# Seven products over four chunks instead of two, in the first gate and up group and the last down group of a SwiGLU layer

## The chip, the cores and the metric

The kernel runs on one core of a Trainium2 chip. The metric is the device time of one execution in microseconds. The kernel before has a median of 1612.01 us over three runs, from 1611.77 to 1614.13.

## The reference, cut to what matters

One layer of a decoder, 256 tokens (T) of width D = 2048, all in fp32. Three token mixers, each with its own branch projection, are merged by gates and go through `w_o`; a SwiGLU layer of inner width FF = 5632 follows:

```python
x = x + merged @ w_o
h2 = rmsnorm(x, ffn_norm)
gate, up = split(h2 @ w_gate_up, 2)      # 2048 -> 2 x 5632
x = x + (silu(gate) * up) @ w_down       # 5632 -> 2048
```

## The kernel before, in words

**A product in fp32.** Each operand is split in two parts that TensorE multiplies fast, high and low: for a weight, `split` casts it on ScalarE (ACT, L151, tile `wh`) and subtracts the cast from it on VectorE (DVE, L152, tile `wl`). A product of a chunk of 128 inputs is then three matmuls, each 128 x 128 by 128 x 512: x high by w high (L268), x high by w low (L270), x low by w high (L271).

**A group.** `sgemm` computes two blocks of 512 output columns (j = 0, 1) for the two tiles of 128 tokens (t = 0, 1), over all chunks of the inner dimension: 16 for gate and up (one gate block and the up block beside it), 12 in the last part of the down product. Weights come by DMA as raw tiles of four chunks, 1 MB each. They are worked on in halves of two chunks: one cast of 128 x 1024, one subtraction, then the matmuls. The six raw tiles and six pairs `wh`, `wl` are rings: a new load waits until an old tile has been read for the last time.

**Seven products.** For the first eight chunks of a group the kernel can use the Strassen–Winograd form. The inner dimension is cut into two times SP = 4 chunks, so that the weights are four raw tiles: 11 and 21 (the two inner halves for block 0), 12 and 22 (for block 1). Seven products instead of eight give the four outputs; in the code they are the steps `p1`, `p2`, `p3`, `q4`, `p5`, `p6`, `p7`. Some of them need sums of activations, the *forms* (tiles `sh`, `sl`), which `make_forms` makes once for the whole product from `hh` and `hl`; others need sums or differences of weights, made in place in the raw tiles. The parameter `p` says how many of the four chunks of each half go this way: with p = 2 only the first two do, and the other two chunks of each raw tile go through the plain product (`rest`, in the lists l21, l22, l11, l12); the chunks after the first eight always do (r0 for block 0, r1 for block 1). One half of a step is 6 matmuls, one half of `rest` is 12, for it serves both token tiles.

**Sums of weights.** `prod` makes them on DVE ahead of the split of a half (L283): `p5` (21, 22), `p6` (21, 12), and `q4` (11, 21) where the group is `late` or not `moved`. Two sums go to the DMA queue of GpSimd (POOL) as accumulating transfers from one raw tile into another: `p6` adds 12 to 22 (L351) for `p7`, and in `moved` groups that aren't `late` `p2` adds 21 to 11 (L331) for `q4`. Both move `p` chunks. Such a transfer waits until the tile that it writes has had its last reader, and the cast that follows waits until it has landed.

**Three orders.** A list `seq` sets the order of the steps. The usual one is the last of the three in the code. In the first group of a product the forms aren't ready at the start, so `late` puts everything that needs none ahead: `p1`, `p2`, the plain halves, all of r0 and one of r1; then `made` runs what is left of the background work (here transposes of the normalized x, L455, L154, L155, and the forms, L418), and then come `p5`, `p6`, `p3`, `p7`, `q4` with the rest of r1 between. Its results go through pieces in SBUF, which L404 adds. The last group of the kernel has an order of its own, `end`: block 0's plain halves early, then `p5`, `p6`, `p2`, `p3`, `p7`, `q4`, and r1 at the very end. From these steps a scheduler makes the order of the instructions on each engine; an engine takes its instructions in that order, so one that waits holds up all behind it.

**Where the two groups stand.** The loop at L1130 runs gate and up groups i = 0 to 3, then the down product over those, then 4 to 7, then 8 to 10. Group i = 0 is `late`. The last down group (`end`) is the one for the last two blocks of the third part. The loop of w_o ahead of the FFN calls the same `sgemm` with p = SP, `late` in its first group.

Of the kernel before, what the change touches and what calls it, by code (L numbers as in the profile page):

```python
# [30 lines left out]
SP = KG  # L31
# [46 lines left out]
def trunk(ctx: ExitStack, tc: tile.TileContext, a, out):  # L78
# [109 lines left out]
    def piece():  # L188

        if kit is not None:  # L190
            return kit.tile([P, NB], F32, tag="cv", name="cv", bufs=8)
        if not halves:
            two = gog.tile([P, 2, NB], F32, name="two", tag="g_og")
            halves.extend([two[:, 1], two[:, 0]])
        return halves.pop()
# [214 lines left out]
    def form_tiles():  # L410
        return [fpool.tile([P, 4, SP, P], F32R, name=f"s{x}", tag=f"s{x}") for x in "hl"]

    def make_forms(parts, place):

        def add(dst, a, b, op=ALU.add):
            dve.tensor_tensor(dst, a, b, op=op)  # L418

        def make():  # L420
            a = {}
            for k in range(2):
                for i in range(2):
                    at = piece()
                    a[i, k] = at[:].rearrange("p (k t) -> p k t", k=SP)
                    n = 0
                    for h, l in parts:
                        m = h.shape[1]
                        lo, hi = max(k * SP, n), min((k + 1) * SP, n + m)
                        if lo < hi:  # L430
                            add(
                                a[i, k][:, lo - k * SP : hi - k * SP],
                                *(x[:, lo - n : hi - n, i * P : (i + 1) * P].bitcast(F32) for x in (h, l)),
                            )
                        n += m
                    yield
            a11, a12, a21, a22 = a[0, 0], a[0, 1], a[1, 0], a[1, 1]
            for f, dst, x, y, op in (
                (1, a21, a22, a21, ALU.subtract),
                (3, a22, a12, a22, ALU.subtract),  # L440
                (2, a12, a21, a12, ALU.subtract),
                (0, a11, a11, a12, ALU.add),
            ):
                add(dst, x, y, op)
                yield
                split(place[0][:, f], place[1][:, f], dst)
                yield
            making.remove(id(place))

        making.add(id(place))  # L450
        background.append(make())
        return place
# [96 lines left out]
    gain, i = {}, 0  # L549
# [439 lines left out]
    def to_chunks(src, n, hi, lo, gain):  # L989


        yield
        for c in range(0, 4, 2):
            p = tmp()
            for q in range(2):
                for t in range(2):
                    i = n + (c + q) * P
                    transpose(p[:, q * T + t * P : q * T + (t + 1) * P], src[t][:, i : i + P])
            if gain is None:
                split(*(x[:, c : c + 2].rearrange("p c t -> p (c t)") for x in (hi, lo)), p[:])  # L1000
            else:
                for q in range(2):
                    i = n // P + c + q
                    split(hi[:, c + q], lo[:, c + q], p[:, q * T : (q + 1) * T], gain[:, i : i + 1])
            yield
# [44 lines left out]
    for b in (2, 1, 0):  # L1050
# [3 lines left out]
        for n0 in range(0, D, 2 * NB):  # L1054
# [19 lines left out]
            for n, g in zip((n0, n0 + NB), gs):  # L1074
# [8 lines left out]
                part = [x[:, n // NB % 2 * 4 : n // NB % 2 * 4 + 4] for x in tm[-1]]  # L1083
# [30 lines left out]
    hs = [(hh[:, k], hl[:, k]) for k in range(KD)]  # L1114
# [13 lines left out]
    sf = make_forms([(hh, hl)], form_tiles())  # L1128
    NF = FF // NB
    for part in (range(0, 4), range(4, 8), range(8, NF)):  # L1130
        fs, tiles = [], []
        for i in part:
            for j, result in sgemm(hs, sf, a["w_gate_up"], (i, NF + i), 4 if i else 2, late=i == 0):
                if j == 0:
                    g = [piece()[:] for t in range(2)]
                    for t in range(2):
                        act.activation(g[t], result(t), AF.Silu, scale=r2[:, t : t + 1])
                    continue
                u = [piece()[:] for t in range(2)]
                for t in range(2):  # L1140
                    dve.scalar_tensor_tensor(u[t], result(t), r2[:, t : t + 1], g[t], op0=ALU.mult, op1=ALU.mult)
            f = [kit.tile([P, 4, T], F32R, name=f"f{x}", bufs=4) for x in "hl"]
            background.append(to_chunks(u, 0, *f, None))
            tiles.append(f)
            fs += [(f[0][:, k], f[1][:, k]) for k in range(4)]
            if len(tiles) == 2:
                sd = main.tile([P, 2, 4, SP, P], F32R, name="sd", tag="resid")
                sd = make_forms(tiles, [sd[:, 0], sd[:, 1]])
        final = part[-1] == NF - 1
        if final:  # L1150

            x2s = [fpool.tile([P, D], F32, tag=f"s{x}", name="x2s") for x in "hl"]
            for t in range(2):
                nc.gpsimd.dma_start(x2s[t][:], x2d[:, t])

        for n0 in range(0, D, 2 * NB):
            blks = (n0 // NB, n0 // NB + 1)
            end = final and n0 + 2 * NB == D
            base = (lambda j: x2s[1][:, n0 + j * NB : n0 + (j + 1) * NB]) if final else None
            for j, result in sgemm(  # L1160
                fs, sd, a["w_down"], blks, 2 if end else SP, row0=4 * part[0], moved=end, base=base, end=end
            ):
                n = n0 + j * NB
                for t in range(2):
                    if not final:
                        v = piece()
                        act.copy(v[:], result(t))
                        nc.gpsimd.dma_start(x2d[:, t, n : n + NB], v[:], accum_op=ALU.add)
                        continue

                    width = NB // 2 if n + NB == D else NB
                    for c in range(0, NB, width):
                        v = x2s[t][:, n + c : n + c + width]
                        dve.tensor_tensor(v, v, result(t)[:, c : c + width], op=ALU.add)
                        q = nc.scalar if (t, n + c + width) == (1, D) else nc.sync
                        q.dma_start(out[t * P : (t + 1) * P, n + c : n + c + width], v)
# [50 lines left out]
```

## Time and profile before

| | |
|---|---|
| median of three runs | 1612.01 us (1611.77 to 1614.13) |
| the profiled execution | 1609.67 us, of it span 1607.9 us |
| TensorE (PE) busy | 1600.4 us, 7204 instructions |
| VectorE (DVE) busy | 1354.9 us (84% of the span) |
| ScalarE (ACT) busy | 1043.8 us (65%) |
| first gate and up group on PE | 913.31 to 957.55 us of the span |
| last down group on PE | 1572.02 to 1603.74 us |

In a timeline row the first number is the start in the span, the second the time (of several alike, from the first one's start to the last one's end), then engine, line, operation, and out<-in; "x3" are three in a row, and what stands in brackets is the idle time before it and what ended it. In a row of windows each engine has its busy time and its number of instructions. For a DMA, "to landing" is the time from its issue until the data is there.

### The profile page before, as it was taken

The numbers are of one execution on the slowest core, as the hardware profiler recorded it, in microseconds if no ns is written. First come the engines' busy times: TensorE is split into PE (matmuls) and PEld (weight loads), VectorE is DVE, ScalarE is ACT, GpSimd is POOL, SyncE is SP. The second block draws the span as 40 slices with busy tenths as digits, with TensorE's granted clock in tenths as the row PEclk, the third lists the DMA queues.
The fourth block names the chain that finished last, engine by engine and source line by source line (L and its number), as shares of the span: only waits on it lengthen the run. The fifth ranks groups of instructions, "written<-read, shape, count | busy, mean of one in ns | idle before, by whom it ended". The sixth has DMA issues, their size and how long they took to land.

```text
span 1607.9 us, 19413 instructions
## 1 busy us (share of the span) xinstructions
PE 1600.4 (100%) x7204; PEld 1315.0 (82%) x7204; DVE 1354.9 (84%) x1544; ACT 1043.8 (65%) x1273; POOL 73.0 (5%) x95
## 2 busy tenths in 40 slices
PE   9999999999999999999999999999999999999998
PEld 7888888888888888888888888888888888888887
DVE  6777788897776788897799998988878988888996
ACT  7765677776764666665656766666666666666663
POOL 0000000000000000000000000000000000110000
PEclk9999999999999999999999999999999999999999
DMA  9765768767556878887757868777898786897684
GB/s 377 299 263 168 233 216 262 216 171 255 197 182 218 263 256 264 265 287 287 238 182 261 272 227 256 260 249 236 258 281 260 219 276 231 250 280 242 201 320 128
DMA packets 66383, 394.18 MB, mean 245 GB/s; under 512 B 7344, under 2 KB 14128, under 8 KB 21488
## 3 DMA queue, kind: packets, MB, share of 16 engines
q1 hardware_dynamic: 51344, 323.31, 52.5%
q0 software_dynamic: 11792, 66.59, 21.7%
q10 hardware_dynamic: 3152, 3.04, 0.6%
q8 instruction: 56, 0.92, 0.2%
q14 instruction: 39, 0.32, 0.1%
HBM read 324.24 MB, written 12.58 MB: 209 GB/s over the span
## 4 chain that ended last, share of the span: by engine, by line
PE 96%; DMA 2%; ACT 1%; DVE 1%; issue 0%; SPq 0%; DVEq 0%; ACTq 0%; POOLq 0%
PE acc L268 19%; PE acc L271 19%; PE acc L270 19%; PE tmp L271 7%; PE tmp L270 7%; PE tmp L268 7%; PE acc L226 5%; PE acc L225 5%; PE acc L224 5%; PE tmp L455 2%; DMA raw<-in_w_down 1%; DMA raw<-raw 0%; PE tmp L693 0%; PE tmp L721 0%; ACT wh L151 0%; DMA raw<-in_w_mem_kv 0%
## 5 line engine op out<-in xcount | busy, mean ns | idle before, releaser
L152 DVE TENSOR_TENSOR wl<-raw,wh 128x1024 fp32r<-128x1024 f32 (+1 forms) x765 | 920.1, 1221 | 209.9 <-ACT wh L151 196.6
L151 ACT CAST wh<-raw 128x1024 fp32r<-128x1024 f32 (+1 forms) x766 | 796.6, 1050 | 442.2 <-PE acc L271 225.5
L268 PE MATMUL acc<-wh,xTh 128*128 128x512 f32 x480 | 190.5, 397 | 0.0
L270 PE MATMUL acc<-wl,xTh 128*128 128x512 f32 x480 | 187.2, 390 | 0.0
L271 PE MATMUL acc<-wh,xTl 128*128 128x512 f32 x480 | 186.9, 390 | 0.0
L268 PE MATMUL acc<-wh,hh 128*128 128x512 f32 x452 | 178.8, 395 | 0.0
L270 PE MATMUL acc<-wl,hh 128*128 128x512 f32 x452 | 176.0, 389 | 0.0
L271 PE MATMUL acc<-wh,hl 128*128 128x512 f32 x452 | 175.0, 390 | 0.0
L283 DVE TENSOR_TENSOR raw<-raw 128x1024 f32<-128x1024 f32 x133 | 161.4, 1221 | 1.1 <-DMA raw<-in_w_down 0.5
L224 PE MATMUL acc<-wh,oh 128*128 128x512 f32 x320 | 126.6, 397 | 0.9 <-ACT wh L151 0.9
L225 PE MATMUL acc<-wl,oh 128*128 128x512 f32 x320 | 125.1, 391 | 0.5 <-DVE wl L152 0.5
L226 PE MATMUL acc<-wh,ol 128*128 128x512 f32 x320 | 124.8, 390 | 0.0
L268 PE MATMUL tmp<-wh,sh 128*128 128x512 f32 x294 | 115.7, 394 | 0.0
L271 PE MATMUL tmp<-wh,sl 128*128 128x512 f32 x294 | 114.7, 390 | 0.0
L270 PE MATMUL tmp<-wl,sh 128*128 128x512 f32 x294 | 114.6, 390 | 0.0
L268 PEld LDWEIGHTS acc<-wh,xTh 128*128 128x128 f32 x480 | 90.2, 188 | 20.7 <-ACT acc L314 3.1
L271 PEld LDWEIGHTS acc<-wh,xTl 128*128 128x128 f32 x480 | 90.1, 188 | 19.0
L270 PEld LDWEIGHTS acc<-wl,xTh 128*128 128x128 f32 x480 | 90.2, 188 | 17.8
L268 PEld LDWEIGHTS acc<-wh,hh 128*128 128x128 f32 x452 | 84.9, 188 | 18.6 <-ACT acc L314 1.0
L271 PEld LDWEIGHTS acc<-wh,hl 128*128 128x128 f32 x452 | 84.8, 188 | 18.0
L270 PEld LDWEIGHTS acc<-wl,hh 128*128 128x128 f32 x452 | 84.9, 188 | 16.8
L268 PE MATMUL acc<-wh,fh 128*128 128x512 f32 x220 | 86.5, 394 | 0.2 <-ACT acc L314 0.2
(311 smaller groups left out, 2322.1 us busy)
## 6 DMA issues: line engine op xcount, KB each, us to landing
raw<-in_w_gate_up SPq DMA_DIRECT2D x88, 1024.0 KB, 6.3
raw<-in_w_in SPq DMA_DIRECT2D x56, 1024.0 KB, 5.8
raw<-raw POOLq DMA_DIRECT2D x52, 1024.0 KB, 8.0
raw<-in_w_gate SPq DMA_DIRECT2D x48, 1024.0 KB, 7.4
raw<-in_w_down SPq DMA_DIRECT2D x44, 1024.0 KB, 7.2
raw<-in_w_o SPq DMA_DIRECT2D x16, 1024.0 KB, 6.2
raw<-in_w_mem_kv SPq DMA_DIRECT2D x14, 1024.0 KB, 10.5
raw<-in_w_br_mem SPq DMA_DIRECT2D x8, 1024.0 KB, 5.6
```

Source lines behind the costliest of these rows:

```text
L151: act.copy(hi, src)
L152: dve.tensor_tensor(lo, src, hi.bitcast(F32), op=ALU.subtract)
L224: pe.matmul(o[t][:], xh[:, s], wh[:, j], start=k == 0, stop=False)
L225: pe.matmul(o[t][:], xh[:, s], wl[:, j], start=False, stop=False)
L226: pe.matmul(o[t][:], xl[:, s], wh[:, j], start=False, stop=k == nk - 1)
L268: pe.matmul(dst[:], xh, wh, start=id(dst) not in begun, stop=False, skip_group_check=True)
L270: pe.matmul(dst[:], xh, wl, start=False, stop=False, skip_group_check=True)
L271: pe.matmul(dst[:], xl, wh, start=False, stop=last, skip_group_check=True)
L283: dve.tensor_tensor(x, x, y, op=ALU.add)
L455: pe.transpose(dst, src, ident)
```

## The change

Two arguments become `SP`, so that p = 4 in every group of the gate and up and the down product: in the first gate and up group (`late`), and in the last down group (`end`, the only one with `moved=True` in that loop).

```diff
-            for j, result in sgemm(hs, sf, a["w_gate_up"], (i, NF + i), 4 if i else 2, late=i == 0):
+            for j, result in sgemm(hs, sf, a["w_gate_up"], (i, NF + i), SP, late=i == 0):
...
             for j, result in sgemm(
-                fs, sd, a["w_down"], blks, 2 if end else SP, row0=4 * part[0], moved=end, base=base, end=end
+                fs, sd, a["w_down"], blks, SP, row0=4 * part[0], moved=end, base=base, end=end
             ):
```

In each of the two groups the steps p1 to p7 now work on two halves instead of one (12 matmuls each instead of 6), and the lists l21, l22, l11 and l12 are empty. That is 6 matmuls fewer a group and three split halves more (14 for the first eight chunks instead of 11). The gate group gets three more sums L283 (one each for p5, p6 and q4), the last group two more (p5 and p6). L351 in both groups and L331 in the last move 1 MB instead of 512 KB.

The first place is ACT at the start of the gate group. `wh_7682` is the cast of the first half of p1 in both; `xr` with `x2` is the sum of squares of the last w_o group. Before:

```order
L151 CAST wh_7740<-raw_7728 128x1024
L1108 ACTIVATE xr_7277,x2_ss_6912<-x2_7242 128x512
L1108 ACTIVATE xr_7275,x2_ss_6912<-x2_7242 128x512
L151 CAST wh_7767<-raw_7765 128x1024
L1108 ACTIVATE xr_7277,x2_ss_6912<-x2_7242 128x512
L151 CAST wh_7830<-raw_7810 128x1024
L151 CAST wh_7682<-raw_7680 128x1024
L151 CAST wh_7850<-raw_7848 128x1024
```

Now:

```order
L151 CAST wh_7734<-raw_7722 128x1024
L1108 ACTIVATE xr_7277,x2_ss_6912<-x2_7242 128x512
L1108 ACTIVATE xr_7275,x2_ss_6912<-x2_7242 128x512
L151 CAST wh_7755<-raw_7753 128x1024
L151 CAST wh_7818<-raw_7798 128x1024
L1108 ACTIVATE xr_7277,x2_ss_6912<-x2_7242 128x512
L151 CAST wh_7838<-raw_7836 128x1024
L151 CAST wh_7682<-raw_7680 128x1024
```

One cast (`wh_7838`, a plain half of r1) and the last L1108 have come between `wh_7818` and `wh_7682`. On TensorE 12 matmuls instead of 24 stand ahead of the first one that uses `wh_7682`.

The second place is DVE in the second half of the gate group. `raw_7680` is weight tile 21, `raw_7728` or `raw_7722` tile 11, `raw_7880` or `raw_7868` tile 22 and `raw_7927` or `raw_7910` tile 12; `sl` is a form. Before, from the sum of p6 on:

```order
L283 TENSOR_TENSOR raw_7680<-raw_7680,raw_7927 128x1024
L152 TENSOR_TENSOR sl_7673<-cv_7808,sh_7672 128x512
L152 TENSOR_TENSOR wl_7944<-raw_7927,wh_7943 128x1024
L152 TENSOR_TENSOR wl_7932<-raw_7680,wh_7931 128x1024
L152 TENSOR_TENSOR wl_7954<-raw_7927,wh_7953 128x1024
L152 TENSOR_TENSOR wl_7972<-raw_7969,wh_7971 128x1024
L152 TENSOR_TENSOR wl_7988<-raw_7880,wh_7987 128x1024
L283 TENSOR_TENSOR raw_7728<-raw_7728,raw_7680 128x1024
```

Now, from the second sum of p5 on:

```order
L283 TENSOR_TENSOR raw_7680<-raw_7680,raw_7868 128x1024
L152 TENSOR_TENSOR wl_7895<-raw_7836,wh_7894 128x1024
L283 TENSOR_TENSOR raw_7680<-raw_7680,raw_7910 128x1024
L152 TENSOR_TENSOR wl_7883<-raw_7680,wh_7882 128x1024
L283 TENSOR_TENSOR raw_7722<-raw_7722,raw_7680 128x1024
L152 TENSOR_TENSOR wl_7915<-raw_7680,wh_7914 128x1024
L283 TENSOR_TENSOR raw_7680<-raw_7680,raw_7910 128x1024
L152 TENSOR_TENSOR wl_7976<-raw_7868,wh_7975 128x1024
L283 TENSOR_TENSOR raw_7722<-raw_7722,raw_7680 128x1024
L152 TENSOR_TENSOR wl_7926<-raw_7680,wh_7925 128x1024
```

There are now two sums for each of p5, p6 and q4. `wl_7976` is the first half of p7, read from tile 22, into which L351 adds; it and a sum of q4 stand ahead of `wl_7926`, the second half of p6. On ACT the casts stand in the same order (`wh_7975` ahead of `wh_7925`), while on TensorE the matmuls of p6 come ahead of those of p7.

The third place is ACT at the end of the last group. `raw_13012` or `raw_13015` is tile 22, `raw_13058` or `raw_13067` tile 11, and `raw_13140` or `raw_13157` the last chunks, r1. Before:

```order
L151 CAST wh_13087<-raw_13027 128x1024
L151 CAST wh_13097<-raw_13027 128x1024
L151 CAST wh_13113<-raw_13012 128x1024
L151 CAST wh_13126<-raw_13058 128x1024
L151 CAST wh_13142<-raw_13140 128x1024
L151 CAST wh_13158<-raw_13140 128x1024
```

Now:

```order
L151 CAST wh_13090<-raw_13041 128x1024
L151 CAST wh_13100<-raw_13041 128x1024
L151 CAST wh_13110<-raw_13015 128x1024
L151 CAST wh_13120<-raw_13015 128x1024
L151 CAST wh_13175<-raw_13157 128x1024
L151 CAST wh_13133<-raw_13067 128x1024
L151 CAST wh_13143<-raw_13067 128x1024
L151 CAST wh_13159<-raw_13157 128x1024
```

p7 (`wh_13110`, `wh_13120`) and q4 (`wh_13133`, `wh_13143`) have two halves each, and a half of r1 (`wh_13175`) is now cast ahead of q4's, which waits for L331.

## The prediction

> **What bounds the kernel now.** I read the page first (busy time, and the chain of waits by engine), then the windows of the two places that change and of one place that already has the new form, then their timelines.
>
> ```profile
> PE 1600.4 (100%) x7204; PEld 1315.0 (82%) x7204; DVE 1354.9 (84%) x1544; ACT 1043.8 (65%) x1273; POOL 73.0 (5%) x95
> PE 96%; DMA 2%; ACT 1%; DVE 1%; issue 0%; SPq 0%; DVEq 0%; ACTq 0%; POOLq 0%
> ```
>
> TensorE (PE) is busy throughout and is 96% of the chain: as a rule a matmul fewer is a matmul's time won. VectorE (DVE) at 84% is an average, so it has to be read at the two places.
>
> ```profile
> core 0: us, PE busy (x) PEld busy (x) DVE busy (x) ACT busy (x) POOL busy (x), PEclk, DMA share, GB/s
> 832.00:874.00 42.00, 42.00 (x197) 34.80 (x195) 38.01 (x41) 26.23 (x34) 2.54 (x5) 1.00 0.74 245
> 913.30:937.00 23.70, 23.70 (x113) 19.46 (x112) 23.46 (x48) 16.26 (x27) 2.47 (x4) 1.00 0.58 170
> 937.00:957.40 20.40, 20.40 (x92) 16.90 (x91) 20.03 (x22) 13.83 (x16) 0.00 (x0) 1.00 0.70 277
> 1572.00:1603.70 31.70, 31.70 (x139) 25.63 (x137) 23.03 (x25) 11.91 (x13) 1.73 (x2) 1.00 0.36 107
> ```
>
> The second and third rows are the first gate and up group, the fourth the last down group, the first row the first group of w_o, which runs the same late order with p = 4 today. In the gate group PE has no gap, but DVE is busy 43.49 of 44.10 us: it is as full as PE. In the last group DVE has 8.67 us free, before the transfers that p6 and p2 start are counted.
>
> **The change part by part.** First the prices.
>
> ```profile
> 913.31 0.39 PE L268 MATMUL acc<-wh,hh 128*128 128x512 f32 x1
> 918.75 0.39 PE L268 MATMUL tmp<-wh,hh 128*128 128x512 f32 x1
> 937.15 0.39 PE L268 MATMUL tmp<-wh,sh 128*128 128x512 f32 x1
> 957.55 0.39 PE L268 MATMUL tmp<-wh,hh 128*128 128x512 f32 x1
> ...
> 1572.02 0.39 PE L268 MATMUL tmp<-wh,fh 128*128 128x512 f32 x1
> 1603.35 0.39 PE L271 MATMUL acc<-wh,fl 128*128 128x512 f32 x1
> ```
>
> These are the start of the gate group, its first matmul of p1, its first of p5, the first of the next group; then the last group's first matmul of p1 and the kernel's last matmul. From p5 to the next group the program has 90 matmuls: (957.55 - 937.15) / 90 = 0.2267 us each, the pitch of PE here.
>
> Removed: each of the two groups loses 6 matmuls (186 to 180 and 138 to 132), 2 x 6 x 0.2267 = 2.7 us if nothing else decides. Added, in each: three split halves (a cast on ScalarE, ACT, L151; a subtraction on DVE, L152), and three sums L283 in the gate group, two in the last. The POOL transfers L351 (one in each) and L331 (in the last) go from 512 KB to 1 MB.
>
> ```profile
> 929.00 1.22 DVE L283 TENSOR_TENSOR raw<-raw 128x1024 f32<-128x1024 f32 x1
> 930.13 0.69 DVE L418 TENSOR_TENSOR cv<-cv 128x512 f32<-128x512 f32 x1
> 939.62 5.76 DVE L152 TENSOR_TENSOR wl<-raw,wh 128x1024 fp32r<-128x1024 f32 x5
> 916.60 2.93 ACT L151 CAST wh<-raw 128x1024 fp32r<-128x1024 f32 x3
> ```
>
> The five in a row give DVE a pitch of (5.76 - 1.22) / 4 = 1.135 us for a sum or a split; a 512-wide operation takes about half of it (0.60 from start to start). The cast's pitch is (2.93 - 1.04) / 2 = 0.945, with 1.04 for a single one in the row at 914.22 below. So the gate group gets 6 x 1.135 = 6.8 us of DVE work where 0.6 us are free, and PE 1.36 us less. That cannot hide.
>
> ```profile
> 930.88 0.89 POOL L351 DMA_DIRECT2D raw<-raw  x1 [13.96 <-DVE cv L418]
> 1577.13 0.87 POOL L351 DMA_DIRECT2D raw<-raw  x1 [30.42 <-DVE raw L283]
> 1585.41 0.85 POOL L331 DMA_DIRECT2D raw<-raw  x1 [7.40 <-DVE wl L152]
> ...
> raw<-raw POOLq DMA_DIRECT2D x3, 512.0 KB, 4.6
> raw<-raw POOLq DMA_DIRECT2D x52, 1024.0 KB, 8.0
> ...
> DMA to landing us min/median/max: 5.5/5.5/5.5
> DMA to landing us min/median/max: 6.9/6.9/6.9
> DMA to landing us min/median/max: 4.6/8.8/10.6
> DMA to landing us min/median/max: 4.5/7.8/9.2
> ```
>
> These are the three 512 KB transfers, both sizes with their median from issue to landing, and four looks at the landing: the one at 930.88, the one of w_o's first group (1 MB, the same place in the same order), all of L351, all of L331. A transfer starts about 0.65 us after the DVE sum that it waits for (930.22 to 930.88). For 1 MB at the two places I take 7.0 us: by the w_o row, since both places have the lighter traffic that goes with it (shares 0.74 there, 0.70 and 0.36 here), under the median of 8.0. Bounds: 4.5 (as if it were still 512 KB) and 10.6.
>
> [...]
>
> Gate group, its start. p1 now takes four chunks, so only 12 matmuls, not 24, stand ahead of its first tmp matmul, while that half's cast still stands second behind an L1108 on ACT, which itself now stands behind one more cast.
>
> ```profile
> 914.22 1.04 ACT L151 CAST wh<-raw 128x1024 fp32r<-128x1024 f32 x1
> 915.97 0.63 ACT L1108 ACTIVATE xr<-x 128x512 f32<-128x512 f32 x1 [0.71 <-DVE x L1107]
> 914.12 1.22 DVE L152 TENSOR_TENSOR wl<-raw,wh 128x1024 fp32r<-128x1024 f32 x1
> ```
>
> Behind the cast of the first row another follows now, up to 916.2, then the L1108 to 916.9 (today it ends at 916.60); two casts behind it end at 916.9 + 2 x 0.945 = 918.8. PE gets there at 913.31 + 12 x 0.2267 = 916.0, held 0.45 by the split that ends at 915.34: it waits 2.4 us, and p1 starts at 918.9 instead of 918.75. From there to p5 both orders have 88 matmuls. So p5 starts at about 937.15 as before: the 12 matmuls (2.7 us) saved ahead are paid back in that wait, and 96 stand behind p5 instead of 90, which without a wait would end at 937.15 + 96 x 0.2267 = 958.9.
>
> Gate group, its middle. In DVE's new order nine operations of 1,024 columns and seven of 512 go from the first sum of p5 on (about 929.25, today 929.00) to the second sum of p6: 9 x 1.135 + 7 x 0.60 = 14.4, to 943.65. The transfer L351 waits for p5's second sum, which ends at 936.85, starts at 937.5 and lands at 944.5. On ACT the cast of p7, which waits for it, stands ahead of the cast for p6's second half, and on DVE p7's split and a sum of q4 stand ahead of that half's split. So: cast 945.6, then three operations on DVE, 945.6 + 3 x 1.135 = 949.0. PE comes to this half 30 matmuls behind p5's start and wants the low part at 937.15 + 32 x 0.2267 = 944.4. The wait is 4.7, with 0.2 of small ones behind it 4.9: end 963.8, against 957.55 **+6.3**. Queued behind that cast are those of p6, r1 and q4, and PE waits for all of them. With DVE alone (no landing awaited) the wait would be 2.7 and the sum +4.1; with a landing of 8.8 it is +8.1. The next group's splits have their lead of 4 to 5 us again by then, so I carry nothing over.
>
> Last group. Here DVE goes from 1573.03 through thirteen long operations (nine splits and four sums) and two short ones to the split that frees p2's chunks:
>
> ```profile
> 1573.03 2.36 DVE L152 TENSOR_TENSOR wl<-raw,wh 128x1024 fp32r<-128x1024 f32 x2
> 1585.57 3.49 DVE L152 TENSOR_TENSOR wl<-raw,wh 128x1024 fp32r<-128x1024 f32 x3
> 1590.02 2.95 ACT L151 CAST wh<-raw 128x1024 fp32r<-128x1024 f32 x3 [3.21 <-DMA raw<-raw]
> 1596.77 0.39 PE L268 MATMUL acc<-wh,fh 128*128 128x512 f32 x1
> ```
>
> 13 x 1.135 + 2 x 0.60 = 16.0, to 1589.0. On the way p6's first split is ready at 1584.4 where PE wants it at 1572.02 + 49 x 0.2267 = 1583.1: 1.2 us. L331 starts at 1589.65 (4.2 later than today's 1585.41) and lands at 1596.65. The third row shows the cast that waits for it today, 1590.02, and the fourth the matmul that uses the result, 1596.77: 4.7 us of cover once cast and split are taken off. That is gone: the cast ends at 1597.7, while q4 is due at 1603.35 - 1.36 - 35 x 0.2267 + 1.2 = 1595.3 (35 matmuls follow its first). Wait 2.4, then 1.0 for the split and 0.55 for the second half's, which stands behind two subtractions of p7. Sum 1.2 + 2.4 + 1.0 + 0.55 - 1.36 = **+3.8**. With a landing of 4.5 the 2.4 is nothing and it is +1.3; with 8.8 it is +5.6.
>
> Sum: 6.3 + 3.8 = +10.1; with both floors +5.4, with both landings of 8.8 +13.7. The profiled execution took 1609.67 (span 1607.9, the rest lies around it), 0.15% under the median of 1612.01; 1609.67 + 10.1 = 1619.8, and on the median 1622.1.
>
> **The rivals.** *All is covered* (the other side: faster by 2.7 us, 1609.3, which is 0.17%). For it speaks w_o's first group, the same late order with p = 4, without a gap on PE. Against it: that stretch leaves DVE 3.99 us free, while the gate group, whose DVE also makes hl and the forms (L155, L418), leaves 0.6. It decides only if the splits ran some 5 us further ahead than today's rows show.
>
> *The transfers land early.* If the 1 MB ones took about the 4.5 of a half, only the DVE waits stay: +5.4, 1617.4. For it: the two places have less traffic than the mean stretch. Against it: the shortest of all L351 is 4.6, and that is a 512 KB one; the only 1 MB row in a like place has 6.9.
>
> *The clock falls in the gap.*
>
> ```profile
> 1604.00:1608.00 4.00, 0.00 (x0) 0.00 (x0) 0.52 (x2) 0.00 (x0) 0.00 (x0) 0.85 0.32 107
> 1.19 4.45 PE L582 MATMUL tmp<-zeros 128*128 128x512 bf16 x10 [1.19 <-DVE zeros L579]
> ```
>
> PE stops at 1603.74; a granted clock of 0.85 over the 4 us means half speed for the last 1.2 us, about 3.1 us after PE went idle. The ten matmuls at the start take 0.43 us each, twice the pitch, for some 4.8 us. A gap over 3.1 us would then cost 2.4 more. In the forecast the 4.7 us wait is broken into 2.6, 0.9 and 1.2 by two matmuls (the cast comes before the split), so it stays under; with a landing of 8.8 the first piece is 4.4, and the sum +13.7 + 2.4 = 1628.1.
>
> [...]
>
> **How the numbers follow.** Forecast 0.70 (1622.1), early landings 0.15 (1617.4), fallen clock 0.07 (1628.1), all covered 0.08 (1609.3). The range of eight in ten goes from a little under the two floors, 1615.5, to between the landings of 8.8 (1625.7) and the fallen clock: 1627.5. A measurement of this kernel tells about 0.2% (3.2 us) from no change. All covered comes out within that, and only a part of it beyond: faster 0.02, same 0.08; the rest is slower, 0.90.
>
> **What would show it.** In the changed profile: a first gap on PE ahead of the gate group's first tmp matmul of 2 to 3 us; gaps ahead of p6's second half there that sum to 4 to 5 us, with ACT idle until a raw DMA has landed; the L351 at 937 to 938 and landed 6.5 to 8 later; in the last group an L331 issued near 1589 plus the shift of some 6, and PE waiting for a cast that waits for its landing. It is wrong if PE shows no gap over 1 us at either place, if the next groups show gaps that I did not carry over, or if the start of the gate group is early by 2 us, which would take about as much off the sum only if the middle followed.

## The result, and the profile after

The changed kernel is slower: 1629.36 us in the median of five runs (1625.81 to 1631.47) against 1611.77 for the kernel before (five runs, 1610.11 to 1614.13), a ratio of 1.0112 with a 95% interval from 1.0101 to 1.0124, some 16 to 20 us. I had predicted 1622.1 and a range up to 1627.5: right in sign, but the loss is 1.7 times what I forecast, and outside the range.

The page of the profiled execution (1629.36 us, span 1627.6) shows that TensorE has 12 instructions fewer, but that the chain of waits is no longer nearly all TensorE:

```profile
PE 1606.0 (99%) x7192; PEld 1316.1 (81%) x7192; DVE 1366.7 (84%) x1555; ACT 1049.4 (64%) x1279; POOL 73.0 (4%) x95
PE 90%; DMA 4%; DVE 3%; ACT 1%; issue 1%; SPq 0%; POOL 0%; ACTq 0%; DVEq 0%; POOLq 0%
```

The same places on the timeline of TensorE: the start of the gate group, its first matmul of p1, its first of p5, the first of the next group's p1; then the first of p1 in the last group and the kernel's last matmul.

```profile
914.36 0.39 PE L268 MATMUL acc<-wh,hh 128*128 128x512 f32 x1
919.99 0.50 PE L268 MATMUL tmp<-wh,hh 128*128 128x512 f32 x1 [2.12 <-ACT wh L151]
939.86 0.39 PE L268 MATMUL tmp<-wh,sh 128*128 128x512 f32 x1
973.35 0.39 PE L268 MATMUL tmp<-wh,hh 128*128 128x512 f32 x1
...
1587.57 0.39 PE L268 MATMUL tmp<-wh,fh 128*128 128x512 f32 x1
1623.04 0.39 PE L271 MATMUL acc<-wh,fl 128*128 128x512 f32 x1
```

| stretch | before, us | after, us | difference | predicted |
|---|---|---|---|---|
| up to the gate group | 913.31 | 914.36 | +1.05 | 0 |
| its start to p1 | 5.44 | 5.63 | +0.19 | +0.15 |
| p1 to p5 | 18.40 | 19.87 | +1.47 | 0 |
| p5 to the next group | 20.40 | 33.49 | +13.09 | +6.3 |
| from there to the last group | 614.47 | 614.22 | -0.25 | 0 |
| the last group | 31.33 | 35.47 | +4.14 | +3.8 |

(The 1.05 us ahead of the group arise in the first 360 us, far from the change, and 0.6 of them in the first 20; runs differ there: this stretch was from 913.0 to 916.2 us long in the profiles below. The stretches add up to the 19.7 us between the two profiled executions; the medians differ by 17.6.) The last group is close to what was predicted. The gate group is not: +14.75 instead of +6.3. The chain of waits in that stretch says where most of it is (start, length, what):

```profile
938.67 1.15 DVE raw L283
...
940.46 10.73 DMA raw<-raw
...
951.29 1.05 ACT wh L151
...
952.37 1.23 DVE wl L152
953.60 1.13 DVE raw L283
954.73 1.15 DVE wl L152
...
955.92 0.80 PE tmp L270
956.72 0.43 PE tmp L271
```

This is the predicted chain link by link: p5's second sum, L351, p7's cast, p7's split, a sum of q4, the split of p6's second half. But the transfer takes 10.73 us where I took 7.0. On TensorE it shows as three waits in a row, ahead of the second half of p6:

```profile
953.34 0.79 PE L268 MATMUL tmp<-wh,sh 128*128 128x512 f32 x1 [6.31 <-ACT wh L151]
954.28 0.79 PE L268 MATMUL acc<-wh,sh 128*128 128x512 f32 x1 [0.15 <-ACT wh L151]
955.92 0.80 PE L270 MATMUL tmp<-wl,sh 128*128 128x512 f32 x1 [0.84 <-DVE wl L152]
```

And the matmuls behind it have a pitch of 0.43 us instead of 0.2267. Windows of the same kernel show that the granted clock had fallen, at two places:

```profile
core 0: us, PE busy (x) PEld busy (x) DVE busy (x) ACT busy (x) POOL busy (x), PEclk, DMA share, GB/s
920.00:921.00 1.00, 1.00 (x7) 0.93 (x8) 1.00 (x3) 0.03 (x1) 0.00 (x0) 0.95 1.00 279
924.00:925.00 1.00, 1.00 (x5) 0.83 (x4) 0.92 (x4) 0.00 (x0) 0.00 (x0) 0.84 0.00 0
951.00:953.00 2.00, 0.00 (x0) 0.00 (x0) 0.63 (x1) 1.71 (x2) 0.00 (x0) 0.65 0.00 0
961.00:962.00 1.00, 1.00 (x4) 0.77 (x4) 1.00 (x2) 0.98 (x1) 0.00 (x0) 0.57 1.03 418
```

The windows of 1 us wholly inside a fall have 0.50 each (921 to 924, and 952 to 961). If the clock is either that or 1.00, the values above give the edges, as an estimate: half from 920.9 (0.95 of that microsecond) to 924.3 (0.84), 3.4 us; and from 951.6 to 961.9, 10.2 us.

### The profile page after: what moved, and what is told of

Its sections match the earlier page's. It is cut to its first block, busy times and chain, and to the rows that moved or that the text cites. A ratio compares the mean times of both kernels' runs of the same rounds, so it can differ in the third digit from the quotient of the medians.

```text
span 1627.6 us, 19405 instructions
## 1 busy us (share of the span) xinstructions
PE 1606.0 (99%) x7192; PEld 1316.1 (81%) x7192; DVE 1366.7 (84%) x1555; ACT 1049.4 (64%) x1279; POOL 73.0 (4%) x95
## 4 chain that ended last, share of the span: by engine, by line
PE 90%; DMA 4%; DVE 3%; ACT 1%; issue 1%; SPq 0%; POOL 0%; ACTq 0%; DVEq 0%; POOLq 0%
PE acc L268 17%; PE acc L270 17%; PE acc L271 17%; PE tmp L270 6%; PE tmp L271 6%; PE tmp L268 6%; PE acc L225 5%; PE acc L226 5%; PE acc L224 5%; PE tmp L455 2%; DMA raw<-raw 2%; DVE wl L152 1%; ACT wh L151 1%; DMA od_mem<-out 1%; DVE raw L283 1%
## 5 line engine op out<-in xcount | busy, mean ns | idle before, releaser
L268 PE MATMUL acc<-wh,hh 128*128 128x512 f32 x440 | 174.7, 397 | 0.0
L270 PE MATMUL acc<-wl,hh 128*128 128x512 f32 x440 | 171.9, 391 | 0.3 <-DVE wl L152 0.3
L271 PE MATMUL acc<-wh,hl 128*128 128x512 f32 x440 | 170.5, 390 | 0.0
L283 DVE TENSOR_TENSOR raw<-raw 128x1024 f32<-128x1024 f32 x138 | 167.2, 1220 | 1.1 <-DMA raw<-in_w_down 0.5
L268 PE MATMUL acc<-wh,fh 128*128 128x512 f32 x208 | 81.9, 395 | 1.7 <-ACT wh L151 1.7
## 6 DMA issues: line engine op xcount, KB each, us to landing
raw<-in_w_mem_kv SPq DMA_DIRECT2D x14, 1024.0 KB, 10.3
```

The lines of the kernel that those rows point to most:

```text
L268: pe.matmul(dst[:], xh, wh, start=id(dst) not in begun, stop=False, skip_group_check=True)
L270: pe.matmul(dst[:], xh, wl, start=False, stop=False, skip_group_check=True)
L271: pe.matmul(dst[:], xl, wh, start=False, stop=last, skip_group_check=True)
L283: dve.tensor_tensor(x, x, y, op=ALU.add)
```

## The experiments

Each kernel was timed against the kernel before on the same chip; "group" is the time from the start of the gate group to the next group's first p1 matmul, 44.25 us before. A wait "from start to start" is the time from the start of one matmul to the start of the next, where 0.23 us is no wait.

### The gate group alone, and the last group alone

```diff
-                fs, sd, a["w_down"], blks, SP, row0=4 * part[0], moved=end, ...
+                fs, sd, a["w_down"], blks, 2 if end else SP, row0=4 * part[0], moved=end, ...
```

> Only the first gate and up group goes by four chunks; the last down group keeps p = 2. My theory after the result: nearly all of the loss is made in this group, 14.75 us in the changed profile (p1's wait with a fallen clock, then p6's wait for the landing of L351 with a second fallen clock), so about +14.5 us over before, 1626. Rival: the two groups share the loss more evenly, as I had predicted (+6.3 here): 1618.

1624.72 us, ratio 1.0091 (1.0075 to 1.0108): +14.2. The group takes 58.48 us, +14.2.

```diff
-            for j, result in sgemm(hs, sf, a["w_gate_up"], (i, NF + i), SP, late=i == 0):
+            for j, result in sgemm(hs, sf, a["w_gate_up"], (i, NF + i), 4 if i else 2, late=i == 0):
```

> Only the last down group goes by four chunks; the first gate and up group keeps p = 2. The predicted term stands in the changed profile at +4.1 us; so about 1615.8, with q4's cast waiting for a transfer that is issued some 17 us after p1's start and takes about 7 us. Rival: the term there was shifted by what came ahead of it, and alone the group costs nothing or gains its 6 matmuls (1610 to 1612).

1610.86 us, ratio 1.0003 (0.9994 to 1.0013): nothing that can be told from no change, so a miss. The last group takes 32.05 us (1572.20 to 1604.25), 0.7 over before instead of 4.1. The medians of the two add to 14.5 and not to the whole of 17.6, which the intervals alone would allow. The traces show another order: with the gate group at p = 2, the scheduler takes p2's first half ahead of p6 in the last group, with both changed only behind it. So L331 is issued 13.17 us behind p1's first matmul (1572.20) here, and 17.72 behind it (1587.57) in the changed kernel:

```profile
1585.37 0.85 POOL L331 DMA_DIRECT2D raw<-raw  x1 [6.05 <-DVE wl L152]
```

```profile
1605.29 0.85 POOL L331 DMA_DIRECT2D raw<-raw  x1 [9.46 <-DVE wl L152]
...
1612.31 2.94 ACT L151 CAST wh<-raw 128x1024 fp32r<-128x1024 f32 x3 [2.04 <-DMA raw<-raw]
```

The first row is the last group alone, the others are the changed kernel, with q4's cast waiting for the landing.

### The whole change, with r1's second half early in the gate group

```diff
-            seq = [a, *l21, b, *l11, *r0, *r1[:1], (made,), g, *l22, *r1[1:2], h, e, ...
+            seq = [a, *l21, b, *l11, *r0, *r1[:2], (made,), g, *l22, h, e, ...
```

(for the gate group only; both groups at p = 4)

> The whole change (both groups by four chunks), with the second half of r1 ahead of p5 in the gate group. The scheduler's order of the last group is here that of the changed kernel (p6 ahead of p2), not that of the last group alone. If the order makes the last group's cost, it costs +4 here and the sum is 4.75 + 4 = +8.8, 1619.4. If the last group costs what it costs alone, the sum is +5.1, 1615.6.

1618.35 us, ratio 1.0049 (1.0034 to 1.0064): +7.7. The interval (5.5 to 10.3) leaves out the sum of the parts alone, 5.1, but barely, and that sum has an interval of its own; the profile is plainer. The last group has the late L331 again and takes 36.54 us, +5.2 (about 1 us more than in the changed kernel: the granted clock was 0.95 over it here, and 1.00 there). So in both kernels in which p2 stands wholly behind p6 the group costs 4 to 5 us, and with the other order 0.7, with the same number of matmuls: the cost goes with the order that the scheduler chose.

### The last group alone, with a half of r1 between p7 and q4

```diff
-            seq = [a, *l21, *r0, g, h, *l22, b, *l11, e, *l12, i, f, *r1]
+            seq = [a, *l21, *r0, g, h, *l22, b, *l11, e, *l12, i, *r1[:1], f, *r1[1:]]
```

> The last group alone by four chunks, with the first half of r1 (12 matmuls, 2.7 us) between p7 and q4. If the cast of q4, which waits for L331, is what costs the 6 matmuls' gain, it is covered now: about 1 us less than the last group alone, 1609.5 to 1610. Rival: nothing there is on the path any more; within 0.5 us of it.

1610.74 us, ratio 1.0000 (0.9990 to 1.0009); the last group takes 31.29 us. The group is 0.8 us shorter than alone, and no shorter than with p = 2. But there was no landing to cover: in the last group alone q4's cast waits for L331, while TensorE comes to q4 at 1595.87 without a wait. Its two waits there are 1.66 us from start to start for a subtraction on VectorE (L316, at 1588.65) and 0.54 for a split of r1. Here the second is gone, and the first, 1.37 us at 1589.9, takes most of the 1.4 us of matmuls saved. So the rival was right, and the time of the whole kernel cannot be told from that of the last group alone.

### The gate group with p7's sum on VectorE

```diff
-            nc.gpsimd.dma_start(q[22][0][:, :p], q[12][0][:, :p], accum_op=ALU.add)
             prod(x0, formed(2), 21, False, (21, 12))
...
-            prod(x0, formed(3), 22, True)
+            prod(x0, formed(3), 22, True, (22, 12))
```

(for the gate group only; tile 12 then stays in use until p7)

> As the gate group alone, but the sum of weights for p7 (tile 12 into tile 22) is made by two sums on VectorE instead of the transfer L351; the order of the other instructions stays nearly the same. Theory of the landing: the split of p6's second half ends after nine operations of 1.135 us behind p5's second sum, near 950 us of the span instead of 955.9; PE waits about 3 us instead of 9, in pieces, and the clock does not fall a second time: 8 us less than the gate group alone, about +6 over before, 1618. Theory of a full VectorE: two more sums on the engine that is full anyway cost what the transfer did or more: +14 to +17, 1626 to 1629.

1619.19 us, ratio 1.0051 (1.0036 to 1.0065): 5.5 us less than the gate group alone, although two sums more stand on the fullest engine. On the timeline of VectorE the split of p7 comes at once, 947.02 in a group that began 2.96 us later than that of the gate group alone:

```profile
945.66 1.22 DVE L283 TENSOR_TENSOR raw<-raw 128x1024 f32<-128x1024 f32 x1
947.02 1.23 DVE L152 TENSOR_TENSOR wl<-raw,wh 128x1024 fp32r<-128x1024 f32 x1
948.17 1.22 DVE L283 TENSOR_TENSOR raw<-raw 128x1024 f32<-128x1024 f32 x1
```

The group takes 50.62 us, 7.9 less than with the transfer (8 less was predicted for the whole time); in the profile 1.6 of it are given back in the groups behind it. So the wait for L351, with the clock that falls behind it (granted 0.84 from p5 to the next group in the gate group alone, 0.94 here), is the larger part of the loss, and a full VectorE is not. But 6.4 us over before remain in the group with no transfer at all, a fall of the clock among them (the 0.94, over 26.72 us).

### The gate group with r1's second half early

The edit is the one above, with the last group at p = 2.

> As the gate group alone, but the second half of r1 (12 matmuls) stands ahead of p5 instead of between p5 and p6. Then the raw tile of r1's first chunks comes free before p5's second sum, its weight load no longer starts in the same microsecond as L351, and on ScalarE the cast of p7 stands behind those of p6. Theory of the collision: L351 lands in about 7 us instead of 10.7, p6 does not wait for it at all, the second fall of the clock is gone; p1's wait at the start stays. About +4 over before, 1616. Rival (VectorE is what is late, wherever the half stands): p6 waits as long as before, within 2 us, because 12 matmuls of cover between p5 and p6 are gone: +12 or more, 1624.

1615.31 us, ratio 1.0028 (1.0019 to 1.0038): +4.75 by the medians, 9.4 us less than the gate group alone. The group itself takes 47.04 us, 2.8 over before; in the profile another 2.3 us lie between it and the last group. L351 is issued at 938.48, and it lands in time, with only one load in sight that was issued seven microseconds earlier:

```profile
raw<-in_w_gate_up SPq DMA_DIRECT2D x1, 1024.0 KB, 4.7
raw<-raw POOLq DMA_DIRECT2D x1, 1024.0 KB, 7.0
```

7.0 us is what I had taken from w_o's first group. The longest wait left behind p5 is 1.24 us from start to start. The edit also moves p7's cast behind those of p6 and brings p5 12 matmuls later, so this run alone does not say which of the three helps.

### Half of a load that starts beside L351

In the changed kernel and in the gate group alone a weight load starts 0.55 us behind L351: the split that frees its tile stands right behind p5's second sum on VectorE.

```profile
940.46 0.89 POOL L351 DMA_DIRECT2D raw<-raw  x1 [22.50 <-DVE raw L283]
941.01 0.33 SPq L262 DMA_DIRECT2D raw<-in_w_gate_up  x1
```

My first try halved the wrong load.

```diff
             n = min(KG, nk - k)
+            if "halfload" in alt and (j, k) == (1, 12):
+                n = 2
```

(it leaves the last two chunks unloaded and multiplies by the two before them twice)

> The gate group alone, but the one weight load that starts in the same microsecond as L351 (the last four chunks of r1) brings two chunks instead of four, 512 KB instead of 1 MB, and the last two chunks are multiplied by the weights of the two before; so those columns are not the reference's. Nothing else moves on any engine. Theory of the collision: the transfer shares the 16 engines with that load; L351 lands about 1.9 us sooner, 8.7 to 9.0 instead of 10.6, and the wait ahead of p6's second half is shorter by as much; the time is about 2 us under the gate group alone, 1622.7 on the same before, more if the clock then stays up longer. Rival (the transfer is slow by itself there): it lands in 10.6 as before, and the time is the same.

1624.39 us, ratio 1.0079 (1.0062 to 1.0096), and L351 landed after 10.7 us as before. That looked like the rival, but the halved load (r1's last four chunks) had been issued at 930.00, 13 us ahead; the load beside L351 was still of 1 MB. The run tells nothing on the collision. The load that matters is the first of the next group:

```diff
             n = min(KG, nk - k)
+            if "half21" in alt and (j, k) == (0, SP):
+                n = 2
...
-                wh, wl = half(q[b][0], g)
+                wh, wl = half(q[b][0], at(b, g))
```

(for the next group only, which so leaves two chunks of tile 21 unloaded, uses the other two twice and sends its L331 in two halves)

> The earlier halved load did not start with L351 (it started 13 us before), so the collision stayed untested. The load that does is the next gate and up group's first, tile 21. Here it brings two chunks instead of four, 512 KB instead of 1 MB, and that group uses these two twice, so its block is not the reference's; its L331 is sent as two transfers. Up to the end of the first gate group every engine has the same order as the gate group alone. Theory of the collision: L351 lands between the 7.0 it takes alone and the 10.6 beside the full load, about 8.8; the cast of p7 comes 1.8 us sooner, and the next group starts about 1.8 us sooner after this group's start. Rival (the transfer is slow there whatever runs beside it): it lands after 10.6 us again.

Both DMAs of that microsecond, with their size and time to landing, in the gate group alone, and then with the load halved:

```profile
raw<-raw POOLq DMA_DIRECT2D x1, 1024.0 KB, 10.6
raw<-in_w_gate_up SPq DMA_DIRECT2D x1, 1024.0 KB, 8.8
```

```profile
raw<-raw POOLq DMA_DIRECT2D x1, 1024.0 KB, 9.5
raw<-in_w_gate_up SPq DMA_DIRECT2D x1, 512.0 KB, 6.5
```

With the order unchanged on every engine, the half that is gone from the load takes 1.1 us off the transfer, somewhat less than the 1.8 expected and well outside what full loads showed (10.6, 10.7, 10.7 and 11.1 in four kernels, one execution each). The wait ahead of p6's second half shrinks by as much, in the gate group alone and then with the load halved:

```profile
952.12 0.79 PE L268 MATMUL tmp<-wh,sh 128*128 128x512 f32 x1 [6.27 <-ACT wh L151]
```

```profile
950.05 0.79 PE L270 MATMUL tmp<-wh,sh 128*128 128x512 f32 x1 [5.11 <-ACT wh L151]
```

So the load beside it does lengthen the transfer, and 7.0 (with none), 9.5 (with half) and 10.6 (with all of it) are what it took at this place, in one execution each. The 7.0 is no single case: L331 of the last group, also 1 MB with no load issued beside it, took 7.0 us in the changed kernel (issued at 1605.29) and in the whole change with r1's second half early (1595.33). The time, 1622.96 us (1.0085, 1.0068 to 1.0102), does not tell a difference of that size.

### The wait filled with matmuls

```diff
+                for i in range(fill if kept is not None else 0):
+                    pe.matmul(x1[:], left[0][0], kept, start=True, stop=True, ...)
+                kept = wh[:, 1]
                 for i in range(2):
                     mm(dst, left[g + i], wh[:, i], wl[:, i], ...)
```

(with fill = 26 in p6 of the gate group)

> The gate group alone, with 26 matmuls into a PSUM tile that nobody reads any more put ahead of p6's second half, where TensorE waits (26 x 0.2267 = 5.9 us of about 6.4). ScalarE and VectorE have the same order up to the end of the group. Theory of the clock: the granted clock does not fall behind this wait, the 13 matmuls that follow take 0.227 instead of 0.43 us, and the gate group alone gets 2.5 us faster although it does more: 1622. Rival: the pitch of 0.43 comes from operands that arrive late, not from the clock; the same time, or 1 us more.

1623.39 us, ratio 1.0078 (1.0063 to 1.0093): 1.3 less than the gate group alone (2.5 expected), which the intervals do not tell apart, though 26 matmuls more are done. In the profile the group takes 55.16 us, 3.3 less than in the gate group alone. What the trace tells is the pitch. TensorE behind the wait, with the wait filled:

```profile
945.71 6.05 PE L286 MATMUL tmp<-wh,sh 128*128 128x512 f32 x26
...
955.15 0.50 PE L270 MATMUL tmp<-wl,sh 128*128 128x512 f32 x1 [2.09 <-DVE wl L152]
955.49 0.39 PE L271 MATMUL tmp<-wh,sl 128*128 128x512 f32 x1
955.72 0.40 PE L268 MATMUL tmp<-wh,sh 128*128 128x512 f32 x1
```

The pitch is 0.23, where the changed kernel had 0.43 in the same matmuls. The operands still come late here (L351 took 11.1 us), and the granted clock is 1.00 over the whole group, so it was the clock and not the operands. And the run gave something that I had not asked for: ahead of p5, where the instructions are those of the gate group alone, the clock did not fall either. Windows from p1's first matmul to p5's, the same 88 matmuls in each: the gate group alone, the one with the filled wait, and the one with the wrong load halved.

```profile
918.91:938.78 19.87, 19.87 (x88) 16.78 (x89) 18.05 (x42) 9.34 (x17) 0.00 (x0) 0.92 0.28 99
```

```profile
920.49:938.75 18.26, 18.26 (x88) 15.30 (x89) 17.88 (x42) 9.37 (x17) 0.00 (x0) 1.00 0.32 106
```

```profile
921.29:942.44 21.15, 21.15 (x88) 17.71 (x89) 18.09 (x42) 9.38 (x17) 0.00 (x0) 0.86 0.19 67
```

18.26, 19.87 or 21.15 us for the same instructions behind the same wait of 5.6 us from the start to p1, with a granted clock of 1.00, 0.92 or 0.86 over them.

### p1's cast ahead of the sums of squares

```diff
-            seq = [a, *l21, b, *l11, *r0, *r1[:2], (made,), g, ...
+            seq = [b, *l11, *r0[:1], a, *l21, *r0[1:], *r1[:2], (made,), g, ...
```

> As the gate group with r1's second half early, and p2, and then one half of r0, stand ahead of p1 in the written order; the scheduler puts the cast of p1's first half ahead of the two L1108. Theory that p1's wait at the start is a cost of its own: that wait (3.2 us) and the clock that falls with it (1.5 us) are gone, and the kernel is 3 to 4.7 us faster than with r1's second half early alone: 1610 to 1612.5. Rival (VectorE is full over the whole group): PE comes to p5 earlier and waits there for sums and splits instead; the time stays within 1.5 us, 1614 to 1616.5.

1615.03 us, ratio 1.0028 (1.0018 to 1.0037), the same as with r1 early alone: the rival was right. The waits at the start of the group are down to 0.84 and 1.15 us from start to start, but TensorE then waits 2.23 at p6, 12 matmuls behind p5's start, for a split, and the clock falls there (granted 0.93 from 938.82 to 962.66, and a pitch of 0.43 from 945.29):

```profile
941.53 0.49 PE L268 MATMUL tmp<-wh,sh 128*128 128x512 f32 x1
943.77 0.50 PE L270 MATMUL tmp<-wl,sh 128*128 128x512 f32 x1 [1.75 <-DVE wl L152]
...
945.72 0.63 PE L271 MATMUL tmp<-wh,sl 128*128 128x512 f32 x1
```

### Two sums less on VectorE

```diff
             prod(x0, formed(2), 21, False, (21, 12))
+            nc.gpsimd.dma_start(q[11][0][:, :p], q[21][0][:, :p], accum_op=ALU.add)
...
-            prod(o[1, 0], single(0, 1), 11, last, (11, 21))
+            prod(o[1, 0], single(0, 1), 11, last)
```

> As the gate group with r1's second half early, but the sums of weights for q4 (tile 21 into tile 11) are made by a POOL transfer of 1 MB behind p6, as in the groups whose forms are ready, instead of two sums on VectorE. Theory of a full VectorE: 2 x 1.135 = 2.3 us less work there, the small waits behind p5 (1.24 and 0.96) shrink or go, and the group ends 1 to 2.3 us sooner: 1613 to 1614.3. What stays is p1's wait at the start. Rival (a transfer more costs what it saves): q4's cast waits for its landing, 1615 to 1617.

1616.88 us, ratio 1.0035 (1.0022 to 1.0049): 1.6 over the same without this edit (the intervals overlap), where 1 to 2.3 less were expected, so a miss. The waits behind p5 did shrink, to one of 0.92 from start to start, but TensorE now stops 2.01 us in the next group. On ScalarE, ahead of what it waits for, a cast waits for a weight load, where no such wait stood before.

```profile
960.67 1.05 ACT L151 CAST wh<-raw 128x1024 fp32r<-128x1024 f32 x1 [3.06 <-DMA raw<-in_w_gate_up]
```

That load does not run beside the second transfer: the transfer was issued at 944.76 and landed 7.0 us later, at 951.7, and only then do these two loads start.

```profile
951.78 0.81 SPq L262 DMA_DIRECT2D raw<-in_w_gate_up  x2
```

The awaited one is the second, issued at 952.21; it took 8.4 us, with four other loads issued from 951.78 to 956.78. The first of the two starts as soon as the transfer has landed, and stands at 948.80 in the version without this edit. So the transfer seems to hold a tile, and with it a load, that then runs beside the awaited one; no run tested that.

> The same for the version in which p1's cast stands ahead of the L1108 (p2 and a half of r0 first in the written order). There the wait had moved from p1 to p5 and p6 (2.23 us at 941.5). Theory of a full VectorE: one sum less stands ahead of the split that PE waits for, 1.1 to 2.3 us less, and with the wait shorter the clock may stay up (1.5 us more): 1611.5 to 1613.5. Rival: 1615, as before.

The same edit on the version with p1's cast early: 1613.78 us, ratio 1.0019 (1.0010 to 1.0029), 1.2 less than without the edit (the intervals overlap) and just above the expected 1611.5 to 1613.5. The wait at p6 is 1.69, and the granted clock of the whole profiled execution is 1.000 (0.999 without the edit); 1.74 us are lost in the next group's transposes. It is the best version with p = 4 in the gate group, and it is still slower than the kernel before. No version tried beats that.

## Why the prediction was right or wrong, point by point

**Which steps failed.** Two terms of the gate group's sum, 6.3 predicted and 14.75 measured: the landing of L351, taken at 7.0 us and measured at 10.73, and the clock, left out of the sum, whose two falls cost 4.0.

**The bound.** Right as far as it goes: more work for the gate group did not hide, and moving waits away ended in others each time (p1's to p6, p6's to the next group). That VectorE alone makes the cost is not shown: two more sums on it in place of the transfer made the kernel faster by 5.5 us, and two fewer changed the time by no more than the intervals allow.

**The start of the gate group.** The wait at p1 came to the tenth: 5.63 us from the start to p1, predicted 5.6. The sentence that p5 then starts as before was wrong by the first fall of the clock, 1.47 us, and since splits that wait for transposes and casts came later with it, p5's second sum ended at 939.8 against 936.85 + 1.05.

**The middle.** The chain was right in every link, and the order on ScalarE and VectorE was the cause (p7's operands ahead of p6's). Wrong was a size: "For 1 MB at the two places I take 7.0 us: by the w_o row". It took 10.7. I had read the mean traffic of the kernel before in such stretches, where in w_o no load starts between 836.62 and 846.42, around a transfer issued at 839.68, and not asked which loads the new order releases: the split behind p5's second sum frees a tile, and its load starts half a microsecond behind L351. My upper bound of 10.6 had the value; the sum didn't use it. The waits at p6 came to 9.0 us (6.71, 0.95, 1.64 and 0.59 from start to start, less four pitches) instead of 4.9: of the difference of 4.1, 3.7 is the landing.

**The clock.** This step failed outright. I had given the fall of the clock 7% and a condition, "A gap over 3.1 us", from the one idle stretch at the kernel's end. It fell twice. The first time TensorE had been idle for no more than 2.12 us at a stretch (2.52 from start to start, and 0.72 five matmuls earlier), so the condition itself was wrong. The second time it stayed down for 10.2 us, and 13 matmuls from 956.51 took 5.46 us instead of 13 x 0.2267 = 2.95: 2.5 us, near the 2.4 at which I had priced it. With the 1.47 at the start of the group it is 4.0 us. So: 6.3 predicted, and 1.5 + 4.1 + 2.5 on top, is 14.4 of the 14.75 measured. The 2.4 was an estimate of mine, half of the 4.8 us with a pitch of 0.43 at the kernel's start; the granted clock is 1.00 there (from 1.00 to 6.00 us of the kernel before), so that stretch shows no fall and no length of one.

How long a gap brings a fall these runs do not show. Behind the same wait of 5.6 us from the start to p1, the granted clock from p1 to p5 was 0.92 in the gate group alone, 0.86 with the wrong load halved, and 1.00 with the wait filled and with the load beside L351 halved. I had read a threshold from one gap, and one gap does not give it.

**The last group.** +3.8 predicted, +4.14 measured, with L331 landing after 7.0 as taken, issued 17.72 us behind p1 (predicted 17.63), and q4's cast waiting for it. The pieces are close too: 1.9, 1.0 and 0.4 us at q4 against 2.4, 1.0 and 0.55; the 1.2 foreseen at p6 is 0.7 at p1 and 0.5 at p6; and some 1.3 lie in small delays that I had not counted. But its reading as the price of p = 4 there was too simple. It goes with the order in which the scheduler puts p2 behind p6, and alone the same edit costs +0.7 us on the trace and nothing measurable in the time.

**The rivals.** "All is covered" and "the transfers land early" did not happen. The time of the "fallen clock" case, 1628.1, is the nearest to the result, partly by luck: it took a landing of 8.8 us at both places and one fall of the clock, where the transfers took 10.7 and 7.0 us and the clock fell twice. That the clock could add 2.4 us behind the long wait at p6 was right; that it needs such a wait was not.

## What to carry to other kernels

When work is added where two engines are full, price each transfer in the new order with the loads that the new order itself releases beside it: here a tile that came free at the same moment meant a load that started 0.55 us behind the transfer, which took 10.7 us instead of the 7.0 that I had priced. A wait on TensorE of some 2.5 us can have two prices: its own length, and in some executions 1.6 or 2.9 us more for a clock that falls behind it (19.87 or 21.15 instead of 18.26 us here). And where a scheduler orders the program, two edits far apart are not two separate terms; each order has to be read with both in place.

## What the runs showed of the hardware that I had not expected

The same instructions behind the same wait took 18.26, 19.87 or 21.15 us in different executions, with the granted clock at 1.00, 0.92 and 0.86. The spread between runs of the changed kernel (1625.81 to 1631.47 in five) goes the same way: the granted clock of the whole run was 0.997 in the fastest and 0.994 in the slowest. That it is wider than before (1610.11 to 1614.13) is not shown by five runs each.

At one place in the program a 1 MB accumulating transfer from SBUF to SBUF took 7.0 us with no load beside it, 9.5 beside a load of 512 KB, and 10.6 to 11.1 beside one of 1 MB that started 0.55 us behind it. That load took 8.8 to 9.3 us there; in the gate group with r1's second half early, a load of 1 MB that had landed before the transfer was issued took 4.7.
